# Queries and keys as one 512-feature product, four low weight tiles by an adding DMA, and the convolution's norm on VectorE

## The chip, the cores and the metric

The kernel runs on one core of a Trainium2 chip. The metric is the device time of one execution in microseconds (us), as the median of the runs. The engines are named as in the profile: PE (TensorE) multiplies matrices, PEld is its weight load, DVE is VectorE, ACT is ScalarE, POOL is GpSimd, and SP issues nearly all DMAs. Lines such as L312 are lines of the kernel before.

## The reference, cut to what matters

The input is 256 tokens of 1024 features, and everything is float32. There are two layers. Each layer runs a SwiGLU feed-forward (1024 to 2816 to 1024), a mixing sub-layer, and a second feed-forward, each behind an RMS norm and added to the residual `x`. The mixing sub-layer projects the normed tokens to 2304 features with one matrix `w_in` and cuts them into four mixers:

- a pooling mixer (256 features): moving averages over 2, 4, 8 and 16 tokens, minus the token, times a small matrix per group
- MoBA attention ("m", 4 heads of 64): with 256 tokens and one block of 256 it is plain causal attention; queries and keys are rotated (RoPE on the first 16 features of a head)
- dilated attention ("d", 4 heads of 64): causal attention whose three branches come down to one softmax with a bias; queries and keys are rotated as well
- a convolution (256 features): `h = a * sigmoid(g)`, 31 causal taps per feature, a layer norm over the 256 features with gain and bias, and SiLU

The four results are set side by side and multiplied by `w_out` (1024 x 1024).

## The kernel before, in words

**Two-part products.** Every float32 weight `W` is used as a high part (`hi`, rounded to fp32r) and a low part (`lo`), and every activation likewise, and a product is three matmuls: hi by hi, hi by lo and lo by hi. A weight "unit" of 128 x 2048 elements (1 MB) comes from memory in two pieces. `prep` (L486) does for each piece: a DMA into a `raw` buffer (`dma`, L315, issued by SP), `hi = copy(raw)` on ACT, and `lo = raw - hi` on DVE. There are four `raw` buffers (`RAW`) and five `hi` and `lo` buffers each (`RING`). A `raw` buffer is free for the next DMA once `lo` has been made from it, and a `hi` or `lo` buffer once PE has used the unit five units back.

**Order of the units in a layer.** 22 gate-and-up units and 16 down units of the first feed-forward, then nine units of `w_in` (`cg` and `ca` for the convolution, `qd` and `kd` for dilated attention, two half units of `v` for both attentions, `qm` and `km` for MoBA, `pu` for pooling), then four units of `w_out`, then the second feed-forward. The units of `w_out` are used in the order of features 4-5 (dilated), 0-1 (pooling), 2-3 (MoBA) and 6-7 (convolution); this text calls them wo0 to wo3. Feature block k of the mixers lies in a tile `mx` with a high part `mixh[k]` and a low part `mixl[k]`.

**Products by tokens.** `by_tokens` (L774) makes a 256-feature product with tokens on the partitions: for each of 8 chunks of the inner dimension and each of 2 token halves, three matmuls that keep an activation tile in the array and stream 256 weight columns. `rope` (L787) calls it once for a set of queries or keys, scales by the RMS norm's column on ACT, rotates with four small DVE operations, transposes with four PE matmuls and copies the result with ACT. The `v` product (L841) is already 512 features wide: it streams 512 columns per matmul.

**Convolution.** Four taps are made as products on ACT and added on DVE, and the other 27 taps of 2 feature blocks are 54 `scalar_tensor_tensor` operations on DVE per layer. Then follow the bias (ACT), the mean over features (PE, result `ln`), the subtraction (DVE), the square over 512 columns (ACT, tile `lsq`), the sum of its two halves (DVE), the sum over features as two one-column matmuls (PE), an inverse square root on DVE, a transposed row copy, the scaling (DVE), gain and bias (two operations on ACT), tanh (ACT), and the split into high and low parts.

**Order of the work.** The program records all operations and `Plan.order` (L170) puts them in one order before anything runs: it works out a latest start for each from costs given by hand, and then plays the queues forward, each engine taking the most urgent operation that would be ready by those costs. A DMA there costs its columns x 0.00142 us plus a latency `lat` of 0.91 us. Every engine then works through its list strictly in that order on the chip, waiting where an operand is late. PSUM banks are dealt out in the order of the program (`place`, L290): four banks in turn for products ("mm"), three for attention ("qk"), one for small sums ("sm").

Of the kernel before, what the change touches and what calls it, by code (L numbers as in the profile page):

```python
# [8 lines left out]
F32 = mybir.dt.float32  # L9
# [7 lines left out]
T = 256  # L17
KC = 8
# [32 lines left out]
LEAD = 6.0  # L51

ALL, BLOCKS = ((0, KC),), ((0, 4), (4, 6), (6, 7), (7, 8))
W_OUT = (4, 0, 2, 6)


# [14 lines left out]
class View:  # L71
# [20 lines left out]

    def rows(self, n=2):
        return self._then(lambda t: t.unsqueeze(1).to_broadcast([128, n, T]))

    def heads(self):
        return self._then(lambda t: t.to_broadcast([128, 2, 4, t.shape[3]]))

    def to_broadcast(self, shape):
        return self._then(lambda t: t.to_broadcast(shape))  # L100
# [163 lines left out]
def trunk(ctx: ExitStack, tc: tile.TileContext, d):  # L264
# [18 lines left out]
    def work(tag, n, shape, name, dt=F32):  # L283
        return plan.buf(wk, shape, dt, turn(tag, n), name)
# [11 lines left out]
    def bank(tag, n, shape, name):  # L296
        i = turns.get(tag, 0)
        turns[tag] = i + 1
        if tag == "qk":
            return place(min(BANKS[tag], key=lambda i: age[i]), shape, name)  # L300
        return place(BANKS[tag][i % len(BANKS[tag])], shape, name)
# [8 lines left out]
    def rec(eng, cost, f, w, r, a, k, lat=0.0):  # L310
        def emit():
            f(*[val(x) for x in a], **{n: val(x) for n, x in k.items()})  # L312
        plan.op(eng, cost, emit, w=w, r=[x for x in r if isinstance(x, View)], lat=lat)

    def dma(out, in_, cols, lat=0.91):  # L315
        rec("sp", max(0.1, cols * 0.00142), nc.sync.dma_start, [out], [], (), {"out": out, "in_": in_}, lat=lat)

    def dma_act(out, in_):
        rec("act", 0.47, nc.scalar.dma_start, [out], [], (), {"out": out, "in_": in_}, lat=1.8)

    def store(out, in_, cols):
        rec("sp", max(0.1, cols * 0.00142), nc.sync.dma_start, [], [in_], (), {"out": out, "in_": in_}, lat=0.91)

    def A(n, out, in_, func, **k):
        w = [out] + ([k["accum_out"]] if "accum_out" in k else [])
        extra = sum(isinstance(k.get(x), View) for x in ("scale", "bias", "accum_out"))
        rec("act", 0.093 + 0.000833 * n + 0.093 * extra, nc.scalar.activation, w, [in_, k.get("scale"), k.get("bias")],
            (out, in_, func), k)
# [9 lines left out]
    def tt(n, name, out, a, b):  # L338
        vec(0.067 + n * 0.001045, name, out, a, b)
# [10 lines left out]
    def ts(n, out, a, s1, s2, op0, op1=None):  # L350
        def f(out, a, s1, s2):
            k = {} if op1 is None else {"op1": op1}
            nc.vector.tensor_scalar(out, a, s1, s2, op0=op0, **k)
        rec("dve", 0.07 + n * 0.00075, f, [out], [a, s1, s2], (out, a, s1, s2), {})
# [30 lines left out]
    def transpose(cost, out, in_):  # L385
        rec("pe", cost, nc.tensor.transpose, [out], [in_, ident], (out, in_, ident), {})
# [10 lines left out]
    def pcol(i):  # L397
        return gain[:, i:i + 1] if i < P_PS else par[:, i:i + 1]
# [17 lines left out]
        Sum().mm(0.4, warm[:, 0:128], (mean_w, mean_w))  # L416


    units, output = [], set()
    for l in range(DEPTH):  # L420
        for w in range(2):
            for f in range(FC):
                units.append((d["gu"][l, w, f], 16))
            for m in range(KC):
                for h in range(2):
                    units.append((d["dn"][l, w, m, :, h * HALF:(h + 1) * HALF], FC // 2))
            if w == 0:
                for k in range(9):
                    units.append((d["wi"][l, k], 16))
                for k in range(4):  # L430
                    output.add(len(units))
                    units.append((d["wo"][l, k], 16))
    made = []

# [51 lines left out]
    def prep():  # L486
        n = len(made)
        src, ch = units[n]
        hi = plan.buf(ring, [128, UNIT], F32R, f"hi{n % RING}", f"hi{n}")
        lo = plan.buf(ring, [128, UNIT], F32R, f"lo{n % RING}", f"lo{n}")  # L490
        parts = 2
        plan.lead = LEAD if n in output else 0.0
        where = []
        for i in range(parts):
            a, b = ch * i // parts, ch * (i + 1) // parts
            where += [i] * (b - a)
            a, b = a * 128, b * 128
            raw = plan.buf(ring, [128, UNIT // 2], F32, turn("raw", RAW), f"raw{n}_{i}")[:, :b - a]
            h, o = hi.on(i)[:, a:b], lo.on(i)[:, a:b]
            dma(raw, src[:, a:b], b - a)  # L500
            A(b - a, h, raw, AF.Copy)
            tt(b - a, "tensor_sub", o, raw, h.bitcast(F32))

        plan.lead = 0.0

        def part(c, n=1):

            s = slice(c * 128, (c + n) * 128)
            return hi.on(where[c])[:, s], lo.on(where[c])[:, s]

        made.append(part)
# [3 lines left out]
    def take():  # L515
        n = used[0]
        used[0] += 1
        while len(made) < min(n + 1, len(units)):
            prep()
        return made[n]  # L520
# [98 lines left out]
    def flat(v):  # L619
        return v.rearrange("p a b -> p (a b)")  # L620
# [46 lines left out]
    def slot(i, name, dt=F32):  # L667

        return plan.buf(act, [128, 2, T], dt, f"slot{i}", name)
# [54 lines left out]
    def mix(l, nrm, after):  # L724
# [49 lines left out]
        def by_tokens(nm):  # L774

            part = take()
            ps = bank("mm", 4, [128, 2, T], f"{nm}{l}")
            s = Sum()
            for k in range(KC):
                w = part(2 * k, 2)  # L780
                for t in range(2):
                    sl = slice(t * 128, (t + 1) * 128)
                    xh, xl = nrm.y[k].on(0)[:, 0, sl], nrm.y[k].on(1)[:, 1, sl]
                    s.mm(0.36, ps.on(t)[:, t], (xh, w[0]), (xh, w[1]), (xl, w[0]))
            return ps

        def rope(i, j, nm, col):  # L787

            ps = by_tokens(nm)
            q = slot(i, f"{nm}t{l}")  # L790
            for t in range(2):
                A(T, q.on(t)[:, t], ps.on(t)[:, t], AF.Copy, scale=col[:, t:t + 1])
            v = q.rearrange("p t (h e) -> p t h e", h=4)
            a = work("ra", 2, [128, 2, 4, 16], f"ra_{nm}{l}")
            b = work("rb", 2, [128, 2, 4, 16], f"rb_{nm}{l}")
            tt(64, "tensor_mul", b.on(0)[:, :, :, 0:8], v[:, :, :, 8:16], sin_t[:, :, :, 0:8].heads())
            tt(64, "tensor_mul", b.on(1)[:, :, :, 8:16], v[:, :, :, 0:8], sin_t[:, :, :, 8:16].heads())
            tt(128, "tensor_mul", a, v[:, :, :, 0:16], cos_t.heads())
            tt(128, "tensor_add", v[:, :, :, 0:16], a, b)
            ps = bank("qk", 2, [128, 2, T], f"tr_{nm}{l}")  # L800
            for t in range(2):
                for c in range(2):
                    transpose(0.09, ps.on(2 * t + c)[:, c, t * 128:(t + 1) * 128], q[:, t, c * 128:(c + 1) * 128])
            out = slot(j, f"{nm}{l}")
            A(512, out, ps, AF.Copy)
            return out

        def scores(q, k, c, bias, nm, place):

# [23 lines left out]
                A(b - a, p.on(t)[:, a:b], s.on(t)[:, a:b], AF.Copy, scale=rd[:, t:t + 1])  # L833
            return p

        qd = rope(8, 14, "qd", qcol)
        kd = rope(9, 15, "kd", nrm.col)
        pd = [p for c in range(2) for p in scores(qd, kd, c, C_BD, f"d{l}", 16)]


        psv = [bank("mm", 4, [128, 512], f"v{l}{t}") for t in range(2)]  # L841
        vt = [flat(slot(20 + t, f"vt{l}{t}")) for t in range(2)]
        sv = [Sum(), Sum()]
        for u in range(2):
            part = take()
            for t in range(2):
                sl = slice(t * 128, (t + 1) * 128)
                for i in range(4):
                    k = u * 4 + i
                    wh, wl = part(4 * i, 4)  # L850
                    xh, xl = nrm.y[k].on(0)[:, 0, sl], nrm.y[k].on(1)[:, 1, sl]
                    sv[t].mm(0.65, psv[t], (xh, wh), (xh, wl), (xl, wh))
        for t in range(2):
            A(512, vt[t], psv[t], AF.Copy, scale=nrm.col[:, t:t + 1])

# [21 lines left out]
                A(T, mixh[k], ps[c], AF.Copy)  # L877
                tt(T, "tensor_sub", mixl[k], ps[c], mixh[k].bitcast(F32))

        qm = rope(8, 23, "qm", qcol)  # L880
        km = rope(9, 24, "km", nrm.col)
        pv(pd, 256, 4, 16, f"d{l}")
        pm = [p for c in range(2) for p in scores(qm, km, c, C_BM, f"m{l}", 16)]

# [35 lines left out]
            sp.mm(0.432, pss[:, 0:T], (mean_w, yv.on(c)[:, c]))  # L920
        tt(512, "tensor_sub", yv, yv, pss[:, 0:T].rows())
        sq = slot(13, f"lsq{l}")
        A(512, sq, yv, AF.Square)
        sq2 = work("acc", 2, [128, T], f"lsq2{l}")
        tt(T, "tensor_add", sq2, sq[:, 0], sq[:, 1])
        ps2 = bank("sm", 1, [128, 512], f"ln2{l}")
        sp = Sum()
        for t in range(2):
            sp.mm(0.15, ps2.on("c")[:, 256 + t:257 + t], (sq2[:, t * 128:(t + 1) * 128], ones[:, 0:1]))
        lcol = rsqrt_cols(ps2.on("c")[:, 256:258], 256.0, 1e-5, f"ln{l}")  # L930
        lrb = row_broadcast(ps2, lcol, f"ln{l}", "lrb")
        tt(512, "tensor_mul", yv, yv, lrb.rows())
        for c in range(2):
            A(T, yv.on(c)[:, c], yv.on(c)[:, c], AF.Identity, bias=pcol(P_LB + 2 * l + c),
              scale=pcol(P_LG + 2 * l + c))
        lth = slot(11, f"lth{l}")
        A(512, lth, yv, AF.Tanh, scale=0.5)
        stt(512, yv, lth, 1.0, yv, ALU.add, ALU.mult)
# [157 lines left out]
```

## Time and profile before

| what | value |
| --- | --- |
| median of 3 runs | 939.41 us (938.25 to 940.3) |
| the profiled execution | 939.43 us, span 937.6 us |
| granted TensorE clock, mean | 0.997 |
| PE busy | 924.9 us (99%) |
| DVE busy | 721.5 us (77%) |
| ACT busy | 563.8 us (60%) |
| POOL busy | 33.3 us (4%) |
| DMA, mean | 181 GB/s |

The span runs from the first to the last instruction; the profiled execution took 1.83 us more than it. A matmul's duration in the profile overlaps with the next one's, so what a matmul costs is read from the distance between two starts, and idle time of PE from the distance to the next start less the usual one. The mixing sub-layer of layer 0 lies at 191 to 282 us, that of layer 1 at 652 to 743 us.

### The profile page before, as it was taken

What the parts mean: (1) busy time and instruction counts of PE and PEld (TensorE: products, weight loads), DVE (VectorE), ACT (ScalarE), POOL (GpSimd) and SP (SyncE); (2) the same over time, 40 slices, a digit from 0 to 9 for tenths busy, and PEclk for the clock granted to TensorE, in tenths of its full rate; (3) what the DMA queues carried; (4) which work ended last, traced back from release to release, by engine and by line L of the source; (5) the groups of instructions that cost most, each with busy time, mean ns of one, the idle gap of its engine ahead of it and who ended that gap; (6) DMA issues with size and microseconds to landing.
All of it is one profiled execution on the core that took longest, in us unless ns stands there. A gap on an engine that the chain in (4) does not pass through costs nothing.

```text
span 937.6 us, 15074 instructions
## 1 busy us (share of the span) xinstructions
PE 924.9 (99%) x5644; PEld 822.4 (88%) x5644; DVE 721.5 (77%) x1329; ACT 563.8 (60%) x1049; POOL 33.3 (4%) x45
## 2 busy tenths in 40 slices
PE   9999999999999999999999999999999999999996
PEld 8888888898998888888888888888988988888885
DVE  6789976679888988765778887667797888886652
ACT  7776655558576676555546565445667776565540
POOL 0000000100002000000000000011000200000010
PEclk9999999999999999999999999999999999999998
DMA  8856566762164756456765554567512576654641
GB/s 301 280 199 214 171 179 199 232 217 93 35 229 156 249 200 209 127 161 195 251 213 181 180 189 137 166 193 253 187 46 96 197 239 212 221 173 125 187 125 45
DMA packets 55210, 170.18 MB, mean 181 GB/s; under 512 B 6368, under 2 KB 8416, under 8 KB 55136
## 3 DMA queue, kind: packets, MB, share of 16 engines
q1 hardware_dynamic: 54704, 168.92, 55.9%
q8 instruction: 44, 0.72, 0.3%
q10 hardware_dynamic: 432, 0.29, 0.1%
q14 instruction: 30, 0.25, 0.1%
HBM read 168.14 MB, written 1.05 MB: 180 GB/s over the span
## 4 chain that ended last, share of the span: by engine, by line
PE 93%; DVE 3%; DMA 2%; ACT 1%; issue 1%; DVEq 0%; SPq 0%; ACTq 0%
PE mm_gu L368 50%; PE dn L368 26%; PE v L368 2%; PE wo L368 2%; PE pu L368 1%; PE qd L368 1%; PE qm L368 1%; PE kd L368 1%; PE km L368 1%; PE mm_cg L368 1%; PE mm_ca L368 1%; DMA raw<-in_gu_dram 1%; DVE lo L312 1%; DVE y_f L346 1%; DMA x<-in_x_dram 1%
## 5 line engine op out<-in xcount | busy, mean ns | idle before, releaser
L312 DVE TENSOR_TENSOR lo<-raw,hi 128x1024 fp32r<-128x1024 f32 (+3 forms) x365 | 387.7, 1087 | 63.1 <-ACT hi L312 47.3
L312 ACT ACTIVATE hi<-raw 128x1024 fp32r<-128x1024 f32 (+3 forms) x365 | 329.6, 938 | 137.3 <-PE dn L368 54.8
L368 PE MATMUL mm_gu<-y_f,hi 128*128 128x512 f32 x1408 | 332.4, 391 | 0.9 <-DVE y_f L346 0.7
L368 PEld LDWEIGHTS mm_gu<-y_f,hi 128*128 128x128 f32 x1408 | 260.7, 188 | 54.8 <-ACT hi L312 1.8
L368 PEld LDWEIGHTS mm_gu<-y_f,lo 128*128 128x128 f32 x1408 | 176.0, 191 | 4.0
L368 PE MATMUL mm_gu<-y_f,lo 128*128 128x256 f32 x1408 | 178.1, 283 | 0.0
L368 PE MATMUL dn<-h,hi 128*128 128x512 f32 x704 | 169.4, 390 | 0.0
L368 PEld LDWEIGHTS dn<-h,hi 128*128 128x128 f32 x704 | 128.7, 188 | 24.1
L312 DVE TENSOR_TENSOR t<-mm_gu,t 128x256 f32<-128x256 f32 x176 | 73.0, 421 | 49.8 <-ACT t L312 47.1
L368 PEld LDWEIGHTS dn<-h,lo 128*128 128x128 f32 x704 | 91.5, 191 | 4.3
L368 PE MATMUL dn<-h,lo 128*128 128x256 f32 x704 | 92.8, 282 | 0.0
L312 ACT ACTIVATE t<-mm_gu 128x256 f32<-128x256 f32 x176 | 64.3, 375 | 30.0 <-PE mm_gu L368 29.9
L312 ACT ACTIVATE h<-th 128x256 fp32r<-128x256 f32 x88 | 36.4, 417 | 63.2 <-DVE th L312 63.1
L312 DVE TENSOR_TENSOR t<-t,rb_f 128x512 f32<-128x512 f32 x88 | 60.2, 686 | 0.9
L312 ACT ACTIVATE th<-t 128x256 f32<-128x256 f32 x88 | 36.5, 415 | 40.3 <-DVE t L312 28.5
L346 DVE SCALAR_TENSOR_TENSOR x<-dn,x 128x256 f32<-128x256 f32 x64 | 27.0, 422 | 38.8 <-PE dn L368 38.2
L368 PE MATMUL wo<-mx,hi 128*128 128x256 f32 x256 | 48.4, 289 | 1.7 <-DVE mx L312 1.7
L346 DVE SCALAR_TENSOR_TENSOR yv<-hpad,par,yv 128x256 f32<-128x256 f32 x108 | 44.0, 478 | 0.0
L312 DVE TENSOR_TENSOR h<-th,h 128x256 fp32r<-128x256 f32 x88 | 36.8, 420 | 7.6 <-ACT h L312 6.8
L368 PEld LDWEIGHTS wo<-mx,hi 128*128 128x128 f32 x256 | 39.9, 191 | 2.3 <-DVE mx L312 2.2
L312 DVE TENSOR_TENSOR th<-th,t 128x256 f32<-128x256 f32 x88 | 36.8, 419 | 5.5 <-ACT th L312 5.1
L368 PE MATMUL wo<-mx,lo 128*128 128x256 f32 x128 | 36.2, 283 | 0.0
(209 smaller groups left out, 674.4 us busy)
## 6 DMA issues: line engine op xcount, KB each, us to landing
raw<-in_gu_dram SPq DMA_DIRECT2D x170, 512.0 KB, 4.5
raw<-in_dn_dram SPq DMA_DIRECT2D x64, 384.0 KB, 3.6
raw<-in_dn_dram SPq DMA_DIRECT2D x64, 320.0 KB, 3.0
raw<-in_wi_dram SPq DMA_DIRECT2D x36, 512.0 KB, 4.7
raw<-in_wo_dram SPq DMA_DIRECT2D x16, 512.0 KB, 3.9
raw<-in_gu_dram SPq DMA_DIRECT2D x9, 256.0 KB, 5.5
con<-in_con_dram SPq DMA_DIRECT2D x1, 932.0 KB, 7.5
x<-in_x_dram SPq DMA_DIRECT2D x3, 256.0 KB, 5.4
```

The lines of the kernel that those rows point to most:

```text
L312: f(*[val(x) for x in a], **{n: val(x) for n, x in k.items()})
L346: nc.vector.scalar_tensor_tensor(out, in0=a, scalar=scalar, in1=b, op0=op0, op1=op1)
L368: nc.tensor.matmul(val(o), lhsT=val(lhsT), rhs=val(rhs), start=self.i == 0, stop=self.i == self.n - 1, skip_group_check=True)
```

## The change

Four edits and one number:

1. `rope` no longer makes one 256-feature product for queries and one for keys. A new function `wide` makes one 512-feature product for both, from two half units of the inner dimension, as `v` was made before; `v` uses the same function. Each token half has its own PSUM bank. Scaling, rotation and transposes are done per token half for queries and keys together, in as many operations as before. The host lays the columns of `w_in` out to match. The set `APART`, which would send units of `w_in` to the adding DMA, is empty, so the pooling's unit keeps its low part on DVE.
2. For the first two units of `w_out` in each layer (wo0 and wo1), `lo` is made by ACT writing `-hi` into it and a DMA issued by POOL that reads the same weights from memory and adds them to it.
3. The square in the convolution's norm is two DVE products of 256 columns in place of one ACT square of 512 and one DVE sum; each half goes to its own pair of one-column matmuls, so there are four in place of two.
4. Gain and bias of that norm are two DVE `tensor_scalar` in place of two ACT operations.
5. The planner's latency for a plain DMA is 1.9 us in place of 0.91 us. It changes the order that is written, over the whole program.

```diff
+APART = ()
@@
-    def dma(out, in_, cols, lat=0.91):
+    def dma(out, in_, cols, lat=1.9):
@@
+    def dma_add(out, in_):
+        rec("pool", 1.2, nc.gpsimd.dma_start, [out], [], (), {"out": out, "in_": in_, "accum_op": ALU.add}, lat=6.0)
@@
                 for k in range(4):
                     output.add(len(units))
+                    if k < 2:
+                        apart.add(len(units))
                     units.append((d["wo"][l, k], 16))
@@
             A(b - a, h, raw, AF.Copy)
-            tt(b - a, "tensor_sub", o, raw, h.bitcast(F32))
+            if n in apart:
+                A(b - a, o, h.bitcast(F32), AF.Copy, scale=-1.0)
+                dma_add(o, src[:, a:b])
+            else:
+                tt(b - a, "tensor_sub", o, raw, h.bitcast(F32))
@@
+        def wide(nm):
+            ps = [bank("mm", 4, [128, 512], f"{nm}{l}{t}") for t in range(2)]
+            sm = [Sum(), Sum()]
+            for u in range(2):
+                part = take()
+                for t in range(2):
+                    sl = slice(t * 128, (t + 1) * 128)
+                    for i in range(4):
+                        y = nrm.y[u * 4 + i]
+                        wh, wl = part(4 * i, 4)
+                        xh, xl = y.on(0)[:, 0, sl], y.on(1)[:, 1, sl]
+                        sm[t].mm(0.68, ps[t], (xh, wh), (xh, wl), (xl, wh))
+            return ps
@@
-        qd = rope(8, 14, "qd", qcol)
-        kd = rope(9, 15, "kd", nrm.col)
+        qd, kd = rope(8, 14, "d")
@@
-        qm = rope(8, 23, "qm", qcol)
-        km = rope(9, 24, "km", nrm.col)
+        qm, km = rope(8, 23, "m")
@@
-        A(512, sq, yv, AF.Square)
-        sq2 = work("acc", 2, [128, T], f"lsq2{l}")
-        tt(T, "tensor_add", sq2, sq[:, 0], sq[:, 1])
@@
-        for t in range(2):
-            sp.mm(0.15, ps2.on("c")[:, 256 + t:257 + t], (sq2[:, t * 128:(t + 1) * 128], ones[:, 0:1]))
+        for c in range(2):
+            tt(T, "tensor_mul", sq.on(c)[:, c], yv.on(c)[:, c], yv.on(c)[:, c])
+            for t in range(2):
+                sp.mm(0.15, ps2.on("c")[:, 256 + t:257 + t],
+                      (sq.on(c)[:, c, t * 128:(t + 1) * 128], ones[:, 0:1]))
@@
-            A(T, yv.on(c)[:, c], yv.on(c)[:, c], AF.Identity, bias=pcol(P_LB + 2 * l + c),
-              scale=pcol(P_LG + 2 * l + c))
+            ts(T, yv.on(c)[:, c], yv.on(c)[:, c], pcol(P_LG + 2 * l + c), pcol(P_LB + 2 * l + c), ALU.mult, ALU.add)
```

## Rows read from the trace of the kernel before

**Rows 1.** Page part 1: busy time, share of the span, instructions.

```profile
PE 924.9 (99%) x5644; PEld 822.4 (88%) x5644; DVE 721.5 (77%) x1329; ACT 563.8 (60%) x1049; POOL 33.3 (4%) x45
```

**Rows 2.** Waits of PE: who waited for whom, total us, times, longest.

```profile
PE wo L368 <- DVE mx L312: 1.7, 2, 0.9
```

**Rows 3.** Windows, layer 0: us, PE, PEld, DVE, ACT, POOL, clock, DMA share, GB/s.

```profile
228.50:240.40 11.90, 11.90 (x101) 11.90 (x100) 11.44 (x32) 5.92 (x8) 0.00 (x0) 1.00 0.00 1
240.40:253.30 12.90, 12.90 (x117) 11.01 (x116) 10.70 (x36) 7.30 (x22) 0.00 (x0) 1.00 0.13 42
```

**Rows 4.** Timeline of PE: start, us, instruction; the v and qm products.

```profile
226.21 0.62 PE L368 MATMUL v<-hi,y_m 128*128 128x512 f32 x2
...
226.89 0.62 PE L368 MATMUL v<-hi,y_m 128*128 128x512 f32 x2
...
228.71 0.40 PE L368 MATMUL qm<-hi,y_m 128*128 128x256 f32 x2
...
229.07 0.40 PE L368 MATMUL qm<-hi,y_m 128*128 128x256 f32 x2
```

**Rows 5.** Timeline of PE: the norm's one-column sums, and the next start.

```profile
263.35 0.61 PE L368 MATMUL ln<-ones,lsq 128*128 128x1 f32 x4
263.81 0.48 PE L368 MATMUL wo<-mx,hi 128*128 128x256 f32 x2
```

**Rows 6.** Timeline of DVE, layer 0: the last taps and the low parts.

```profile
242.29 5.23 DVE L346 SCALAR_TENSOR_TENSOR yv<-hpad,par,yv 128x256 f32<-128x256 f32 x13
...
248.14 1.22 DVE L312 TENSOR_TENSOR lo<-raw,hi 128x1024 fp32r<-128x1024 f32 x1
...
266.17 2.36 DVE L312 TENSOR_TENSOR lo<-raw,hi 128x1024 fp32r<-128x1024 f32 x2
...
269.04 1.22 DVE L312 TENSOR_TENSOR lo<-raw,hi 128x1024 fp32r<-128x1024 f32 x1
270.18 0.75 DVE L312 TENSOR_TENSOR mx<-pv_m,mx 128x256 fp32r<-128x256 f32 x2
...
272.69 0.75 DVE L346 SCALAR_TENSOR_TENSOR mx<-yv,mx 128x256 fp32r<-128x256 f32 x2
```

**Rows 7.** Timeline of ACT, layer 0: the high parts, and MoBA's result.

```profile
229.26 3.90 ACT L312 ACTIVATE hi<-raw 128x1024 fp32r<-128x1024 f32 x4
...
265.69 0.65 ACT L312 ACTIVATE mx<-pv_m 128x256 fp32r<-128x256 f32 x2
```

**Rows 8.** Timeline of PE: wo's start and its wait, layer 0.

```profile
253.37 0.59 PE L368 MATMUL wo<-mx,hi 128*128 128x256 f32 x2
...
269.50 0.28 PE L368 MATMUL wo<-mx,hi 128*128 128x256 f32 x1
270.65 0.38 PE L368 MATMUL wo<-mx,hi 128*128 128x256 f32 x1 [0.87 <-DVE mx L312]
```

**Rows 9.** Timeline of PE: the second feed-forward's start, layer 0.

```profile
282.15 1.25 PE L368 MATMUL mm_gu<-y_f,hi 128*128 128x512 f32 x3
283.78 1.43 PE L368 MATMUL mm_gu<-y_f,hi 128*128 128x512 f32 x5 [0.38 <-DVE y_f L346]
...
296.69 3.81 PE L368 MATMUL mm_gu<-y_f,hi 128*128 128x512 f32 x16
300.92 0.43 PE L312 MATMUL st_f<-ident,y_f 128*128 128x128 f32 x2 [0.42 <-DVE y_f L346]
```

**Rows 10.** Page part 6: DMA issues, count, KB each, median us to landing.

```profile
raw<-in_wi_dram SPq DMA_DIRECT2D x36, 512.0 KB, 4.7
```

**Rows 11.** Groups of DVE and ACT by shape: busy, mean ns, idle before.

```profile
L312 DVE TENSOR_TENSOR lsq<-lsq 128x256 f32<-128x256 f32 x2 | 0.9, 426 | 4.6 <-ACT lsq L312 4.6
L312 ACT ACTIVATE lsq<-yv 128x512 f32<-128x512 f32 x2 | 1.2, 623 | 0.0
```

**Rows 12.** Timelines of POOL and DVE side by side, layer 0.

```profile
283.97 4.26 POOL L312 TENSOR_TENSOR acc_f<-acc_f,sq_f 128x256 f32<-128x256 f32 x5 [0.53 <-ACT sq_f L312]
284.31 3.32 DVE L346 SCALAR_TENSOR_TENSOR y_f<-x,gain,y_f 128x256 fp32r<-128x256 f32 x4
```

More of the change, by code (lines that the diff above doesn't have):

```diff
@@ L94, in rows @@
         return self._then(lambda t: t.unsqueeze(1).to_broadcast([128, n, T]))
-    def heads(self):
-        return self._then(lambda t: t.to_broadcast([128, 2, 4, t.shape[3]]))
     def to_broadcast(self, shape):
@@ L416, in trunk @@
         Sum().mm(0.4, warm[:, 0:128], (mean_w, mean_w))
-    units, output = [], set()
+    units, output, apart = [], set(), set()
     for l in range(DEPTH):
@@ L428, in trunk @@
                 for k in range(9):
+                    if k in APART:
+                        apart.add(len(units))
                     units.append((d["wi"][l, k], 16))
@@ L431, in trunk @@
                     output.add(len(units))
+                    if k < 2:
+                        apart.add(len(units))
                     units.append((d["wo"][l, k], 16))
@@ L785, in by_tokens @@
             return ps
-        def rope(i, j, nm, col):
-            ps = by_tokens(nm)
-            q = slot(i, f"{nm}t{l}")
-            for t in range(2):
[L792 to L800, printed above, removed]
-            for t in range(2):
[L802 to L806, printed above, removed]
+        def wide(nm):
[11 more added lines that the diff above has]
+            return ps
@@ new lines, in rope @@
+        def rope(i, j, nm):
+            ps = wide(f"qk{nm}")
+            out = [bank("qk", 2, [128, 2, T], f"tr_{n}{nm}{l}") for n in "qk"]
+            for t in range(2):
+                qk = flat(slot(i + t, f"qk{nm}t{l}{t}"))
+                for n, col in enumerate((qcol, nrm.col)):
+                    s = slice(n * T, (n + 1) * T)
+                    A(T, qk.on(n)[:, s], ps[t][:, s], AF.Copy, scale=col[:, t:t + 1])
+                v = qk.rearrange("p (h e) -> p h e", h=8)
+                a = work("ra", 2, [128, 8, 16], f"ra_{nm}{l}{t}")
+                b = work("rb", 2, [128, 8, 16], f"rb_{nm}{l}{t}")
+                sin, cos = sin_t[:, t], cos_t[:, t]
+                tt(64, "tensor_mul", b.on(0)[:, :, 0:8], v[:, :, 8:16], sin[:, :, 0:8].to_broadcast([128, 8, 8]))
+                tt(64, "tensor_mul", b.on(1)[:, :, 8:16], v[:, :, 0:8], sin[:, :, 8:16].to_broadcast([128, 8, 8]))
+                tt(128, "tensor_mul", a, v[:, :, 0:16], cos.to_broadcast([128, 8, 16]))
+                tt(128, "tensor_add", v[:, :, 0:16], a, b)
+                for n in range(2):
+                    for c in range(2):
+                        f = n * T + c * 128
+                        transpose(0.09, out[n].on(2 * t + c)[:, c, t * 128:(t + 1) * 128], qk[:, f:f + 128])
+            res = []
+            for n in range(2):
+                res.append(slot(j + n, f"{'qk'[n]}{nm}{l}"))
+                A(512, res[n], out[n], AF.Copy)
+            return res
@@ L834, in softmax @@
             return p
-        qd = rope(8, 14, "qd", qcol)
-        kd = rope(9, 15, "kd", nrm.col)
+        qd, kd = rope(8, 14, "d")
         pd = [p for c in range(2) for p in scores(qd, kd, c, C_BD, f"d{l}", 16)]
-        psv = [bank("mm", 4, [128, 512], f"v{l}{t}") for t in range(2)]
+        psv = wide("v")
         vt = [flat(slot(20 + t, f"vt{l}{t}")) for t in range(2)]
[L843 to L852, printed above, removed]
         for t in range(2):
@@ L922, in mix @@
         sq = slot(13, f"lsq{l}")
-        A(512, sq, yv, AF.Square)
-        sq2 = work("acc", 2, [128, T], f"lsq2{l}")
-        tt(T, "tensor_add", sq2, sq[:, 0], sq[:, 1])
         ps2 = bank("sm", 1, [128, 512], f"ln2{l}")
         sp = Sum()
-        for t in range(2):
-            sp.mm(0.15, ps2.on("c")[:, 256 + t:257 + t], (sq2[:, t * 128:(t + 1) * 128], ones[:, 0:1]))
+        for c in range(2):
+            tt(T, "tensor_mul", sq.on(c)[:, c], yv.on(c)[:, c], yv.on(c)[:, c])
+            for t in range(2):
+                sp.mm(0.15, ps2.on("c")[:, 256 + t:257 + t],
+                      (sq.on(c)[:, c, t * 128:(t + 1) * 128], ones[:, 0:1]))
         lcol = rsqrt_cols(ps2.on("c")[:, 256:258], 256.0, 1e-5, f"ln{l}")
@@ L1053 @@
     plw = np.zeros((DEPTH, 128, 2, 128), f32)
-    cols = [16, 17, 14, 15, 8, 9, 10, 11, 2, 3, 4, 5, 0, 1]
+    cols = [16, 17, 14, 15, 0, 1]
     for l in range(DEPTH):
@@ L1060 @@
         win = I["w_in"][l].reshape(KC, 128, 18, 128)
-        wi[l, [0, 1, 2, 3, 6, 7, 8]] = (win[:, :, cols].reshape(KC, 128, 7, 2, 128).transpose(2, 1, 0, 3, 4)
-                                        .reshape(7, 128, UNIT))
-        wi[l, 4:6] = win[:, :, [6, 7, 12, 13]].reshape(2, 4, 128, 512).transpose(0, 2, 1, 3).reshape(2, 128, UNIT)
+        wi[l, [0, 1, 8]] = (win[:, :, cols].reshape(KC, 128, 3, 2, 128).transpose(2, 1, 0, 3, 4)
+                            .reshape(3, 128, UNIT))
+        for u, four in ((2, [8, 9, 10, 11]), (4, [6, 7, 12, 13]), (6, [2, 3, 4, 5])):
+            wi[l, u:u + 2] = win[:, :, four].reshape(2, 4, 128, 512).transpose(0, 2, 1, 3).reshape(2, 128, UNIT)
         wot = I["w_out"][l].reshape(KC, 128, KC, 128)
```

## The prediction

> **What bounds the kernel now.** I read the page's busy shares first: PE has work in 99% of the span, no other engine in more than 77% [rows 1]. Next the waits of PE, to see whether that 99% is matmuls or waiting: the longest entry of the view is 1.7 us, in two pieces, one in each layer, where `w_out` waits for a low part of the mixers' result [rows 2]. So the time is nearly the sum of what PE has to issue, and an edit pays only if it shortens PE's stream or removes one of these few waits. Relief of DVE or ACT by itself is worth nothing.
>
> Then the timeline of PE at those places, start to start. A 256-column matmul starts every 0.12 us (three from 228.71 to 229.07), and a 512-column one every 0.227 us (three from 226.21 to 226.89) [rows 4]. In layer 0, `w_out` starts a matmul at 269.50, could start the next at 269.62 and starts it at 270.65: 1.03 us lost [rows 8]. The two entries of that wait are equal to within 0.1 us, so I take 1.03 us for layer 1 as well. At the start of layer 0's second feed-forward two more stretches are lost: 283.78 in place of 282.15 + 3 x 0.227 = 282.83, which is 0.95 us, and 300.92 in place of 296.69 + 16 x 0.227 = 300.33, which is 0.59 us [rows 9].
>
> Last, the windows, DVE and ACT, for the reason of the wait. From 228.5 to 240.4 no DMA runs at all (1 GB/s), and up to 253.3 hardly one (42 GB/s), while DVE is busy for 11.4 us of 11.9 [rows 3]: the taps run until 247.5, so the low parts of wo0 and wo1, whose high parts ACT began at 229.26, are made only from 248.14 on [rows 6, 7]. The four `raw` buffers stay taken till then, so the loads of wo2 and wo3 start after 249. Their low parts then fall at 266 to 270, ahead of MoBA's `mixl` on DVE: ACT had finished that result's high part at 266.3 [rows 7], and DVE comes to the low part at 270.18, after three weight tiles [rows 6]. That is the 1.03 us.
>
> **Queries and keys in one product.** Per layer, four 256-feature units are 4 x 8 x 2 x 3 = 192 matmuls at 0.12 us = 23.04 us. Now they are two products of 2 x 8 x 3 = 48 matmuls of 512 columns, 96 in all at 0.2267 us = 21.76 us. That removes 1.28 us a layer, **2.56 us** in all; both durations are read from this kernel's own products with the same kind of operands, so I give it only 0.2 us either way. Transposes (16 a layer), scalings, rotations and copies keep their number and size. The product of 512 needs two of the four product banks at once instead of one after the other. Going through the order in which banks are dealt out, these are the same banks as before, last used by the feed-forward's late down products, so nothing new waits there. Queries and keys of MoBA now end together, and their rotation lies behind the product; PE has the pooling's product and, once the dilated result is in, wo0 to fill that with.
>
> **Norm of the convolution.** PE gets two more one-column products per layer. Two cost 0.46 us (263.35 to 263.81) [rows 5]. If the halves are issued together the second two cost less than that, if wo's matmuls lie between, the same: 0 to 0.46 us, and I take 0.4, **0.8 us** in all. On DVE two products of 256 columns, 0.43 each by the nearest row, replace one sum of the same price, and ACT loses a square of 0.62 [rows 11]. No row shows a `tensor_scalar` of 256 columns; between nothing and a tap's 0.40 (5.23 / 13) [rows 6] the two cost 0 to 0.8 us of DVE, and I take 0.8, as the tap is the nearest. None of it is on the path: wo3, which alone needs the convolution, starts 5.76 us before 282.15, at 276.4 [rows 9], and its low parts were done by 273.5 [rows 6].
>
> **Adding DMAs.** DVE loses four tiles of 1.2 us per layer [rows 6]. ACT gains four copies; with 0.97 us for a high part (3.90 / 4) [rows 7] these end near 237, in a window where ACT is busy for half the time [rows 3]. `raw` is now free when the high part is done, at 230 to 233 in place of 249 and later, so wo2 and wo3 load in the empty window, and their low parts take the places on DVE which those of wo0 and wo1 leave. Then MoBA's low part has no weight tile of `w_out` ahead of it, and can follow its high part at 266.3 + 0.75 = 267.1, before PE asks for it at about 268.3 (269.62 less 1.28). What is late next is the gate-and-up weights, which are due only at 282. I count the wait as gone: 1.03 us a layer, **2.06 us**. The bounds are 0 (another tile is put there) and 2.06. The extra reading is 8 x 512 KB, in windows that moved 1 to 42 GB/s. No row shows an adding DMA or one issued by POOL. From below it costs nothing, if it lands in time. From above, see the rival on it. What queues behind it on POOL is only the next one: POOL's other work in the layer starts at 282.
>
> **The planner's latency.** It changes what order is written, not what is done. In the feed-forwards PE shows no wait beyond those named, so nothing can be won there but 0.95 + 0.59 us at layer 0's second start, and a new order may add waits like the present ones, about 1 us each. I take 0.
>
> **Sum.** Against the profiled execution's 939.43 us (span 937.6 and 1.83 around it, practically the median of 939.41): 939.43 - 2.56 + 0.80 - 2.06 = 935.6 us.
>
> **Rivals.** *Only PE's own stream changes.* The wait stays, or the new order puts an equal one elsewhere: 939.43 - 2.56 + 0.80 = 937.7 us, and with a further 1 us per layer 939.8. For it speaks that each list is written from costs given by hand, and that the present wait already contradicts the plan. Against it speaks that the tiles in its way have 15 us more to go elsewhere.
>
> *More goes.* Loads that run two units earlier also take away both waits at layer 0's second start, where DVE idles for late loads: 935.6 - 1.54 = 934.1 us, and 933.3 with the extra one-column products at nothing. Against it: the first of these waits hangs on the residual's chain on DVE as well, beside POOL's sums.
>
> *The adding DMAs come too late, and it gets slower.* Rows show POOL and DVE shutting each other out: while POOL adds, four `y_f` operations of DVE take 3.32 us, 0.83 each, where a tap, of the same kind and size, takes 0.40, and POOL's five take 0.85 each [rows 6, 12]. If making a DMA's descriptors on POOL is shut out in the same way while the taps fill DVE, the four begin only at 247.5. One after another at the 4.7 us of a plain 512 KB load [rows 10] the last lands at 247.5 + 18.8 = 266.3. PE wants that tile, wo1's second half, near 262.6: wo0 and half of wo1 are 24 triples of 0.36 us from 253.4 [rows 8], that is 262.0 less 1.28, and up to 4 us later for the transposes, attention and sums between them. It decides from 3.8 us per transfer. At 4.7 PE loses 3.7 us a layer, and the sum becomes 935.6 + 7.4 = 943.0 us. If they begin when ACT has written the first negative, at 232, they have 7.6 us each, and a plain load fits easily.
>
> The Trainium skill's page "SBUF — State Buffer", section "SBUF: two separate sides", warns of this: descriptors of a DMA issued by GpSimd can't be written while VectorE holds the shared port pair in a two-port mode, but an operation with two SBUF inputs excludes only a GpSimd operation that reads SBUF. By the rule's first half alone the 943.0 of this rival would hold, by both halves the taps, which have two SBUF inputs, let the descriptors through, and 935.6 stands. Rows 12 agree with the part on two inputs, since POOL's sums do read SBUF; no run here shows descriptors.
>
> **Chances.** Forecast 0.45, more goes 0.15, only PE's stream 0.30, too late 0.10. The range runs from 933.0 (nearly all of the second rival) to 940.0 (the first with its further waits) and leaves out little but the last rival. A difference under 0.2% (1.9 us) can't be told from none here. Faster than 937.5: all but a little of the first two cases and a quarter of the third, 0.67. Within 0.2%: 0.22, nearly all of it from the third. Slower than 941.3: 0.11, the last case and a little.
>
> **What would show it.** PE's start-to-start distance in the merged product near 0.227 us, 96 matmuls a layer where there were 192. Eight records of the one-column sums per layer where there were four. DMA traffic between 230 and 245 where there was none, and low parts of wo2 and wo3 before 262. No entry of `w_out` waiting for `mx` among PE's waits. An adding DMA that lands before 250. Wrong would be: `w_out` waiting for its weights, new waits of PE at the first units of a feed-forward, or a distance of over 0.235 us in the merged product.

## The result, and the profile after

The changed kernel takes 945.53 us, median of nine runs (939.76 to 947.16), beside 939.46 for the kernel before (938.25 to 940.33): a ratio of 1.0055, 95% interval 1.0035 to 1.0075. It is slower by 6.1 us; the prediction was 935.6. The profiled execution took 947.04 us (span 945.3).

Page part 1 after, to lay beside [rows 1]: PE has 184 instructions fewer, and yet more busy time, in a longer span.

```profile
PE 928.7 (98%) x5460; PEld 818.0 (87%) x5460; DVE 716.9 (76%) x1327; ACT 570.0 (60%) x1051; POOL 39.5 (4%) x53
```

Waits of PE after (who waited for whom, us in total, times, longest), to lay beside [rows 2]:

```profile
PE qk_m L382 <- DVE mx L311: 5.2, 2, 2.8
```

The wait of `wo` for `mx` is gone, as predicted. In its place MoBA's scores (`qk_m`) wait for VectorE's step on the dilated result, once in each layer. The timeline of PE around it in layer 0 (start, us, instruction, idle time before and its releaser):

```profile
248.58 0.49 PE L382 MATMUL qk_m<-km,qm 64*128 64x128 f32 x2
251.49 1.65 PE L382 MATMUL qk_m<-km,qm 64*128 64x128 f32 x6 [2.42 <-DVE mx L311]
...
255.29 1.65 PE L382 MATMUL qk_m<-km,qm 64*128 64x128 f32 x8
...
259.93 1.02 PE L370 MATMUL psp<-pl,plw 128*128 128x256 f32 x4
```

The first score has a bank; the second head's bank is the one that still holds the dilated result `pv_d`. Then the windows of the same stretch (us, PE, PEld, DVE, ACT, POOL, clock, DMA share, GB/s); the first two answer to [rows 3]:

```profile
228.50:240.40 11.90, 11.90 (x60) 10.05 (x59) 11.87 (x30) 11.51 (x16) 3.44 (x4) 1.00 0.72 203
240.40:253.30 12.90, 10.48 (x82) 8.91 (x81) 8.97 (x27) 7.65 (x14) 0.19 (x1) 0.91 0.93 222
249.00:252.00 3.00, 0.58 (x4) 0.51 (x5) 0.99 (x3) 2.33 (x5) 0.00 (x0) 0.83 0.95 187
252.00:255.00 3.00, 3.00 (x15) 2.35 (x11) 2.92 (x14) 1.67 (x7) 0.00 (x0) 0.50 0.04 7
255.00:258.00 3.00, 3.00 (x22) 2.11 (x23) 1.03 (x7) 1.09 (x5) 0.00 (x0) 0.53 0.00 0
258.00:261.00 3.00, 3.00 (x27) 2.67 (x23) 3.00 (x8) 2.59 (x12) 0.00 (x0) 1.00 0.00 0
```

Two things are to be seen. The DMA engines, which stood still there before, are full. And PE, busy again from 251.49 on, has a granted clock of 0.50 for the next six microseconds, 1.2 in place of 2.4 GHz: eight `qk_m` last 1.65 us, where they last 0.93 in a run that does not stop (below). So the stop is paid twice.

Why the dilated result is late, from the chain that ended last (start, us, what), in layer 0 and in layer 1:

```profile
238.37 11.26 DMA raw<-in_wo_dram
...
251.01 0.44 DVE mx L311
```
```profile
702.43 11.53 DMA raw<-in_wo_dram
...
715.35 0.44 DVE mx L311
```

and ACT's own list there:

```profile
245.86 1.06 ACT L311 ACTIVATE hi<-raw 128x1024 fp32r<-128x1024 f32 x1 [1.19 <-DMA raw<-in_wo_dram]
249.65 1.06 ACT L311 ACTIVATE hi<-raw 128x1024 fp32r<-128x1024 f32 x1 [2.74 <-DMA raw<-in_wo_dram]
250.61 0.64 ACT L311 ACTIVATE mx<-pv_d 128x256 fp32r<-128x256 f32 x2
```

PE had finished `pv_d` by 247. In ACT's written order the high parts of wo2 and wo3 stand ahead of the copy of `pv_d`, and the last of them waits for a plain load issued at 238.37 that takes 11.26 us. PE waits for no weight in either layer; what is late is the copy of `pv_d`, which needs no weight and only stands behind one in ACT's list. DMA traffic of 228 to 254 us, by queue (packets, MB, share of the 16 engines), and by issue (KB each, median us to landing):

```profile
q0 software_dynamic: 576, 2.10, 40.6%
q1 hardware_dynamic: 864, 3.15, 37.9%
...
raw<-in_wo_dram SPq DMA_DIRECT2D x6, 512.0 KB, 7.9
lo<-in_wo_dram POOLq DMA_DIRECT2D x4, 512.0 KB, 13.3
```

An adding DMA (q0) holds the engines for 40.6 / 2.10 = 19.3% of this window per MB, a plain one (q1) for 37.9 / 3.15 = 12.0%.

### The profile page after: what moved, and what is told of

Same layout as the page of the kernel before. It is cut to its first block, busy times and chain, and to the rows that moved or that the text cites. A ratio compares the mean times of both kernels' runs of the same rounds, so it can differ in the third digit from the quotient of the medians.

```text
span 945.3 us, 14713 instructions
## 1 busy us (share of the span) xinstructions
PE 928.7 (98%) x5460; PEld 818.0 (87%) x5460; DVE 716.9 (76%) x1327; ACT 570.0 (60%) x1051; POOL 39.5 (4%) x53
## 4 chain that ended last, share of the span: by engine, by line
PE 90%; DMA 4%; ACT 3%; DVE 1%; issue 0%; DVEq 0%; SPq 0%; ACTq 0%
PE mm_gu L370 51%; PE dn L370 26%; PE wo L370 5%; DMA raw<-in_wo_dram 4%; PE qkd L370 2%; PE mm_cg L370 1%; PE mm_ca L370 1%; PE qk_m L382 1%; ACT hi L311 1%; ACT s_d L311 1%; DVE yv L348 1%; DMA x<-in_x_dram 1%; PE v L370 0%; PE ln L370 0%; ACT gt L311 0%
## 5 line engine op out<-in xcount | busy, mean ns | idle before, releaser
L311 DVE TENSOR_TENSOR lo<-raw,hi 128x1024 fp32r<-128x1024 f32 (+3 forms) x357 | 378.4, 1083 | 67.0 <-ACT hi L311 50.6
## 6 DMA issues: line engine op xcount, KB each, us to landing
lo<-in_wo_dram POOLq DMA_DIRECT2D x8, 512.0 KB, 13.3
```

## The experiments

Ratios are against the kernel before in the same batch (medians 939.02, 939.58 and 939.39 us), with 95% intervals.

**Tell the planner how late the loads are.** All instructions of the change; only the latency by which the written order is made differs for the loads of wo2 and wo3.

```diff
-            dma(raw, src[:, a:b], b - a)
+            dma(raw, src[:, a:b], b - a, 12.0 if n in output and n not in apart else 1.9)
```

> The changed kernel with one number: the planner is told 12 us in place of 1.9 for the plain loads of wo2 and wo3. On ACT their four high parts then stand behind the dilated result; DMAs, sizes and counts are the same. Collision theory: loads still land about 11 us late and the adding DMAs still take about 13 us, but PE does not wait at qk_m, clock 0.997, 933 to 937 us. Order theory, or adding DMAs that are late themselves: 942 to 947 us.

935.38 us (935.16 to 935.92), ratio 0.9960 (0.9948 to 0.9973). ACT and PE in layer 0:

```profile
245.59 0.39 ACT L311 ACTIVATE mx<-pv_d 128x256 fp32r<-128x256 f32 x1 [1.40 <-PE pv_d L382]
...
246.52 1.05 ACT L311 ACTIVATE hi<-raw 128x1024 fp32r<-128x1024 f32 x1
```
```profile
247.75 0.93 PE L382 MATMUL qk_m<-km,qm 64*128 64x128 f32 x8
249.87 0.93 PE L382 MATMUL qk_m<-km,qm 64*128 64x128 f32 x8
...
253.34 1.02 PE L370 MATMUL psp<-pl,plw 128*128 128x256 f32 x4
```

The adding DMAs are as slow as before (14.5 us to landing, median, and 274 GB/s from 243 to 246 us), but the copy of `pv_d` now stands ahead of the high parts of wo2 and wo3. From the first `qk_m` to `psp` it is 5.59 us here and 11.35 in the changed kernel, 5.58 and 11.68 in layer 1. Those 11.9 us account for the difference of the two profiled executions (947.04 and 935.32, 11.7 us). Of them 2.42 + 2.81 are idle time, and the remaining 6.6 are as many matmuls of the same sizes, at the low clock.

**Is it the adding or the reading?** The four DMAs a layer copy plainly in place of adding, so the subtraction is left out and the low tiles of wo0 and wo1 hold the weights themselves; every engine's list is the same.

```diff
-        rec("pool", 1.2, nc.gpsimd.dma_start, [out], [], (), {"out": out, "in_": in_, "accum_op": ALU.add}, lat=6.0)
+        rec("pool", 1.2, nc.gpsimd.dma_start, [out], [], (), {"out": out, "in_": in_}, lat=6.0)
```

> The changed kernel with a plain copy in place of the add in the DMAs that POOL issues (so the low parts of wo0 and wo1 hold the weights themselves). If adding is what fills the DMA engines: landing falls from 13.3 us to 4 to 7, the loads of wo2 and wo3 land in under 6 us, no wait at qk_m, 934 to 938 us. If the extra bytes or POOL's issuing do it: landing stays over 10 us and the time at 942 to 947 us.

934.77 us (934.54 to 935.47), ratio 0.9954 (0.9940 to 0.9967). The windows of 243 to 246 us, first here, then after, and the queues of 228 to 254 us here:

```profile
243.00:246.00 3.00, 3.00 (x27) 2.87 (x28) 3.00 (x9) 2.94 (x5) 0.00 (x0) 1.00 1.10 410
```
```profile
243.00:246.00 3.00, 3.00 (x29) 2.72 (x28) 3.00 (x9) 1.81 (x4) 0.00 (x0) 1.00 1.07 274
```
```profile
q1 hardware_dynamic: 864, 3.15, 38.3%
q0 software_dynamic: 576, 2.10, 21.9%
```

The engines are as full, but move 410 GB/s in place of 274: the same bytes from POOL cost 21.9% in place of 40.6%, 1.85 times less. With the same written order ACT reaches `pv_d` at 247.92, 2.7 us earlier, and PE does not stop:

```profile
246.96 1.06 ACT L311 ACTIVATE hi<-raw 128x1024 fp32r<-128x1024 f32 x1 [1.02 <-DMA raw<-in_wo_dram]
247.92 0.64 ACT L311 ACTIVATE mx<-pv_d 128x256 fp32r<-128x256 f32 x2
```
```profile
248.91 0.93 PE L382 MATMUL qk_m<-km,qm 64*128 64x128 f32 x8
```

So the adding makes the difference between a stop and none. It is not the whole of the delay: the second reading costs something too, since plain copies beside the same loads fill the engines as well. The time came out as expected, the landings did not: the copies land after 9.7 us (median, expected 4 to 7), and the plain loads beside them take up to 8.9 us, with the last one at 8.2 in place of 11.26. In the kernel before the loads of `w_out` took 3.1 to 5.0.

**One adding unit in place of two.**

```diff
-                    if k < 2:
+                    if k < 1:
```

> The changed kernel with the adding DMA for one unit of w_out in each layer in place of two (two adding DMAs a layer in place of four); the second unit keeps its low part on VectorE, and the raw buffers of the later units come free behind it. Theory (four adding DMAs and the plain loads fill the 16 DMA engines together, and ACT's written order puts the high parts of those loads ahead of the dilated result): here no high part of wo2 or wo3 stands ahead of the dilated result on ACT, so no stop of PE at qk_m, clock 0.995 or above, and about the forecast, 935 to 938 us. Rival (any adding DMA in this window delays what lies beside it, in proportion): half of the loss, a stop of 1.2 us a layer at qk_m and 940 us.

937.29 us (935.76 to 938.47), ratio 0.9979 (0.9970 to 0.9988). No stop: all eight `qk_m` of the first pair run as one group at 248.44, and ACT copies `pv_d` at 246.28. That is what the theory expected. It does not by itself part the adding from the order, since this kernel has another written order too: no high part of wo2 or wo3 stands ahead of the copy.

**The adding DMAs without the merged product.** The kernel before with edit 2 alone.

> The kernel before with the adding DMAs alone (0.91 us in the planner, products and norm as before). Collision theory: the high parts of wo2 and wo3 stand ahead of the dilated result on ACT here too, so PE waits 1 to 4 us a layer and the time is 941 to 947 us. Order theory: the adding DMAs are harmless, 936 to 939.5 us.

943.20 us (942.41 to 944.29), ratio 1.0043 (1.0030 to 1.0057). PE waits at other places, for the same reason: ACT's copies of `km` and of the dilated scores stand behind high parts whose loads are late by 2.45 and 1.90 us.

```profile
246.26 0.55 PE L312 MATMUL pt_d<-ident,p_d 128*128 128x128 f32 x3 [1.78 <-ACT km L312]
249.98 0.87 PE L383 MATMUL pv_d<-pts_d,vt 128*64 128x256 f32 x8 [0.94 <-ACT pts_d L312]
```

**The change without the adding DMAs.**

```diff
-                    if k < 2:
-                        apart.add(len(units))
```

> The changed kernel without the adding DMAs: wo0 and wo1 get their low parts on DVE again; merged products, norm on DVE and the planner's 1.9 us stay. Collision theory (the adding DMAs slow the plain loads of wo2 and wo3, ACT waits for these ahead of the dilated result, PE stands still and then runs at 1.2 GHz): no wait of PE at qk_m, granted clock 0.997, 935 to 938.5 us. Order theory (the list written with 1.9 us and merged products is worse in itself): the wait at qk_m of 2 to 3 us a layer stays, 942 to 947 us.

941.35 us (939.80 to 943.82), ratio 1.0026 (1.0015 to 1.0037). There is no stop at `qk_m`, but the gain does not come that the first expectation promised; the result lies between the two. **The merged product alone** (edit 1, with the old norm and the old latency) tells the same:

> The kernel before with the merged products of queries and keys alone (0.91 us, DVE low parts, old norm). By PE's stream alone: 2.56 us less, 936.5 us. By what the run without the adding DMAs showed (low parts of wo0 late behind the taps, PE without work at psp and pt_m): 938.5 to 942 us.

944.28 us (943.22 to 948.56), ratio 1.0063 (1.0045 to 1.0081), above both expectations. PE in layer 0:

```profile
252.48 1.13 PE L370 MATMUL psp<-pl,plw 128*128 128x256 f32 x4 [0.84 <-ACT pl L311]
254.79 0.55 PE L311 MATMUL pt_m<-ident,p_m 128*128 128x128 f32 x3 [1.18 <-DVE yv L348]
...
256.39 0.39 PE L370 MATMUL wo<-mx,lo 128*128 128x256 f32 x1 [0.81 <-DVE lo L311]
```

Queries and keys of MoBA now end together, and PE is through the pooling's product when their scores are still on DVE and ACT. `w_out` should fill that time, but wo0's low part is made on DVE only after the taps, at 255.1. The run without the adding DMAs has the same three waits. By these traces the two edits need each other: with the orders written here, the merged product pays only when wo0's low part comes from elsewhere. Whether another order could make it pay alone was not tried.

The run without the adding DMAs shows one thing more. In layer 0 its clock falls as well, with no wait over 1.2 us, and stays at 0.50 for nearly 7 us; in layer 1 the waits of 0.84 and 1.18 us are the same, and it stays at 1.00. That execution is the longest of the seven; the shortest, 939.80 us at a mean clock of 0.997, shows no gain either.

```profile
252.85 1.13 PE L370 MATMUL psp<-pl,plw 128*128 128x256 f32 x4 [0.84 <-ACT pl L311]
255.16 0.90 PE L311 MATMUL pt_m<-ident,p_m 128*128 128x128 f32 x3 [1.18 <-DVE yv L348]
```
```profile
255.00:256.00 1.00, 0.84 (x4) 0.84 (x5) 1.00 (x3) 1.00 (x6) 0.00 (x0) 0.50 0.00 0
```

**The latency alone** (edit 5 on the kernel before).

> The kernel before with 1.9 us in place of 0.91 us in the planner and nothing else. If the new order is worse in itself: 940 to 943 us. If it is neutral or takes the waits at layer 0's second feed-forward away: 937 to 939.5 us.

937.88 us (937.33 to 938.84), ratio 0.9985 (0.9976 to 0.9994). Both entry waits of layer 0's second feed-forward [rows 9] are gone; `wo`'s wait for `mx` stays at 1.8 us in two. I had priced this edit at nothing; alone it is worth 1.7 us (0.6 to 2.3 by the interval).

**The norm alone** (edits 3 and 4 on the kernel before).

> The kernel before with nothing but the convolution's norm moved to VectorE. By the forecast's terms: two more one-column matmuls a layer at 0.33 to 0.4 us, so 0.7 to 0.8 us more: 939.5 + 0.75 = 940.2 us, ratio 1.0008. Rival (VectorE is the engine behind the wait of w_out for MoBA's low part, and two 256-column products, two tensor_scalar operations less one sum, about 1.1 us a layer, are put ahead of it): w_out's wait grows from 0.9 to about 2 us a layer, 942 us. Other rival (ACT is relieved and nothing is lost): 939.5 us.

938.23 us (937.16 to 940.52), ratio 0.9993 (0.9984 to 1.0002): no difference that can be told. PE's extra one-column products are there, and the order written for the new costs has no `wo` wait among PE's waits, but one of 1.0 us for a feed-forward's norm sum (`st_f`), where before had 0.4. The expectation that nothing is lost (939.5) fits; the forecast's term of 0.75 us (ratio 1.0008) lies outside the interval, and the growing wait of `wo` did not come.

**Is the low clock a result of the stop?** First try: six products whose result nobody reads, after MoBA's first pair of scores.

```diff
+            if nm[0] == "m" and c == 0:
+                plan.hold = len(plan.ops) - 1
+                fl = bank("sm", 1, [128, 512], f"fill{l}")
+                fs = Sum()
+                for _ in range(6):
+                    fs.mm(0.432, fl[:, 0:T], (mean_w, con[:, 0:T]))
+                plan.hold = None
```

> The changed kernel plus six idle products per layer (constants into a free bank) between the first and second pair of MoBA's scores, where PE stood still for 2.4 to 2.8 us. They add up to 5 us of PE issue in two layers. If the fall of the clock to 1.2 GHz behind the stop is what makes the loss large: granted clock back to 0.997, PE at 2.4 GHz behind the scores, 938 to 941.5 us although work was added. If the stop alone counts: 945 to 951 us.

951.20 us (948.92 to 953.56), ratio 1.0126 (1.0109 to 1.0144). A miss: the stop lies inside the first pair, so the idle products stood behind it and only added work. Second try: the same six products inside the pair, ahead of the matmul that waits; all other instructions stand where they stood.

```diff
-            together(0.85, *[(sm[e], ps[e][:, 0:128], qa[e][:, 0:128], ka[e][:, 0:128]) for e in range(2)],
+            idle = []
+            if nm[0] == "m" and c == 0:
+                fl = bank("sm", 1, [128, 512], f"fill{l}")
+                fs = Sum()
+                idle = [(fs, fl[:, 0:T], mean_w, con[:, 0:T])] * 6
+            together(0.85, (sm[0], ps[0][:, 0:128], qa[0][:, 0:128], ka[0][:, 0:128]), *idle,
+                     (sm[1], ps[1][:, 0:128], qa[1][:, 0:128], ka[1][:, 0:128]),
```

> The changed kernel with six idle products of 128x256 (float32, result unused, about 0.43 us each, 2.6 us a layer) issued at the very place where PE stops for the bank of pv_d, between the first and the second matmul of MoBA's first pair of scores; every other instruction of every engine stands where it stood. Theory (the stop of 2.4 and 2.8 us lets the granted clock fall, and the low clock costs as much again): PE has work in the stop, the clock stays at 0.995 or above and psw's and wo's matmuls after it run at their usual pitch; although 5.2 us of work is added, the time falls from 945.5 to 939 to 942 us. Rival (the stop itself is the whole loss and the clock falls for another reason): same time as the changed kernel or up to 1 us more, 945 to 947 us, with the clock at 0.5 in 252 to 258 as before.

941.53 us (939.72 to 944.29), ratio 1.0023 (1.0014 to 1.0033): with work added, 4.0 us less than the changed kernel.

```profile
248.46 0.49 PE L382 MATMUL qk_m<-km,qm 64*128 64x128 f32 x2
248.88 2.86 PE L382 MATMUL fill<-con,mean_w 128*128 128x256 f32 x12
252.04 0.92 PE L382 MATMUL qk_m<-km,qm 64*128 64x128 f32 x6 [0.31 <-DVE mx L311]
...
257.62 1.02 PE L370 MATMUL psp<-pl,plw 128*128 128x256 f32 x4
```
```profile
255.00:258.00 3.00, 3.00 (x32) 2.80 (x31) 3.00 (x15) 3.00 (x12) 0.00 (x0) 1.00 0.00 0
```

(Each idle product stands as two records.) The matmul starts at 252.04, no earlier than before, but the clock stays at 1.00 and `psp` starts 9.16 us after the first score in place of 11.35. The mean clock is 0.995 or above in all eleven executions, where seven of the nine of the changed kernel lie below. So the stop is what brought the clock down. The Trainium skill says on its page "TensorE: Matmul & The Clock Gate", section "What's actually happening", that the slow clock is the default and activity lifts it; the two traces, 0.50 behind the stop and 1.00 behind the idle products, agree.

**The best version**: the first experiment with the old norm.

> late_known with the norm of the kernel before (square on ACT, two one-column sums, gain and bias on ACT). The two extra one-column sums cost PE 0.33 us a layer by the changed kernel's row (8 records in 0.79 us against 4 in 0.46), and nothing of the norm is waited for: 0.7 us under late_known, 934.7 us. If the norm's move to DVE kept a wait away: 935.5 to 938 us.

934.81 us (934.41 to 935.04), ratio 0.9951 (0.9939 to 0.9963). It beats both kernels, by 4.8 us and 10.7. Against the first experiment that is 0.6 us, or 1.1 when each is taken against the kernel before of its own batch; the intervals of the two ratios overlap.

## Why the prediction was wrong

**The step that failed** is the price of the adding DMAs: "The extra reading is 8 x 512 KB, in windows that moved 1 to 42 GB/s. ... From below it costs nothing, if it lands in time." The landing was in time: wo0 and wo1 kept PE waiting nowhere. What cost time were the transfers beside them: in place of nothing, the adding DMAs cost PE a stop of 2.42 us in layer 0 and 2.81 in layer 1. I asked only whether the new transfers would be late, and not what they do to the loads beside them, although the same paragraph had put those loads (wo2 and wo3) into the same window. Per layer, four adding and six plain transfers meet there, since the two of wo1, which had begun at 218.65 us, now begin at 230.15; the loads of wo2 and wo3 are issued between 232.4 and 238.4, where I had 230 to 233. The last plain one takes 11.3 us where 4.7 had been the usual [rows 10]. And I looked for those who wait for a load only on PE. The one who waited was ACT, whose list is worked through in order, with the copy of `pv_d` behind. The experiments with the same instructions in another order (935.38) and with plain copies (934.77) show both halves. On the first half, the Trainium skill's page "DMA: Bandwidth & Descriptors", section "Issuing engines are not separate DMA queues", states that whoever issues, the transfers run on the same 16 engines. The trace agrees: with both queues in flight the share is 0.93 to 1.07. My signs of being wrong did not catch this case. `w_out` did not wait for its weights, the merged product kept its pitch, and at the starts of the feed-forwards only the program's first shows a little more waiting, 0.9 us for 0.3.

**The clock** had no place in the working. The stop's 5.2 us became 11.9 in the profiled execution. The runs spread accordingly: 939.76 us was the one with a mean clock of 0.997, 947.16 one with 0.990.

**The rival "too late"** named the right sign and the right edit, but its mechanism is refuted. POOL issued the four while the taps filled DVE, at 0.86 us or a little more each:

```profile
233.56 1.91 POOL L311 DMA_DIRECT2D lo<-in_wo_dram  x2 [47.09 <-DVE yv L348]
236.97 0.86 POOL L311 DMA_DIRECT2D lo<-in_wo_dram  x1 [1.50 <-ACT lo L311]
239.73 0.86 POOL L311 DMA_DIRECT2D lo<-in_wo_dram  x1 [1.90 <-ACT lo L311]
```

Of the Trainium skill's rule weighed in the prediction, the half on operations with two SBUF inputs agrees with these rows: the taps let the descriptors through. The half on a two-port mode is not tested by any run here. My mark of 3.8 us per transfer was no help, since they overlap: each takes 13.3, and PE did not wait.

**Right**: the merged product. Its pitch is the forecast 0.227 us, three from 203.82 to 204.50:

```profile
203.82 0.39 PE L370 MATMUL qkd<-lo,y_m 128*128 128x512 f32 x1
204.05 0.62 PE L370 MATMUL qkd<-hi,y_m 128*128 128x512 f32 x2
204.50 0.39 PE L370 MATMUL qkd<-lo,y_m 128*128 128x512 f32 x1
```

The one-column sums take 0.82 us (270.33 to 271.15) where two took 0.46 [rows 5], 0.36 a layer for my 0.4:

```profile
270.33 0.95 PE L370 MATMUL ln<-ones,lsq 128*128 128x1 f32 x8
271.15 0.48 PE L370 MATMUL wo<-mx,hi 128*128 128x256 f32 x2
```

`wo`'s wait is gone, 2.06 us. The rival "more goes" was right on layer 0's second start: both waits are gone. The latency of edit 5 is enough for that by itself; the adding DMAs by themselves take them away too, and put two like them (0.45 and 0.47 us) at layer 1's second start. By these terms the sum is 939.43 - 2.56 + 0.72 - 2.06 - 1.54 = 934.0 us; the first experiment, which has 0.8 us of `wo`'s wait back, comes to 935.3 in its profiled execution. So the terms that I priced from rows held, and the one that I let stand at nothing because its window was empty took them all back and more. The norm's 0.72 us is read from PE's rows alone; the run with the norm alone does not show it in the time.

**Open**: whether the norm's move costs anything by itself, since each edit also writes a new order (935.38 against 934.81 with it, 938.23 against 939.39 for it). Why the clock fell in most executions and not in all is not settled either. The length of a stop alone does not decide it: it stayed up after 2.20 us in the first filler kernel's layer 1 and fell after 2.42 to 2.81, but in the run without the adding DMAs it fell after waits of 0.84 and 1.18 us in one layer and not after the same waits in the other.

## What to carry to other kernels

An empty window is a price of nothing only for the first transfer in it: when an edit both adds transfers and frees buffers, add up all that will now run there, and ask of each load who stands behind its consumer on an engine that works in order. A stop of PE of a few microseconds is to be priced with the slow clock that may follow. Where an order is written from costs given by hand, correct the cost that the edit makes wrong before judging the edit: here one latency was worth 10 us.

## What the runs showed of the hardware

- A DMA that adds into SBUF took the 16 engines 1.85 times as long per byte as a plain one from the same queue (40.6 against 21.9% of 26 us for 2.10 MB); with them in flight the window moved 274 GB/s, with plain copies in their place 410.
- Plain 512 KB loads beside four such transfers landed after up to 11.8 us, beside four plain copies from the same queue after up to 8.9; the adding ones landed after 13.3 (median), the copies after 9.7.
- In the profiled executions, stops of PE of 2.42 and 2.81 us were followed by nearly 7 us at 1.2 GHz, one of 2.58 by 3.4, one of 2.20 by none; waits of 0.84 and 1.18 us, one soon after the other, were followed by nearly 7 us of it in one layer and by none in the other. 2.9 us of idle products in the place of the stop kept 2.4 GHz.
